# Convolution and 2x2 maximum on one core: head rows through casting loads, joint row sums, and another program order

## The chip, the core and the metric

One of the eight cores of a Trainium2 chip runs the kernel. Its engines work side by side, each through its own queue in order: PE (TensorE, products into PSUM; PEld is its weight load), DVE (VectorE), ACT (ScalarE), POOL (GpSimd) and SP (SyncE, which here only starts transfers). A wait at the head of a queue holds up all that stands behind it on that engine. The metric is the device time of one execution in microseconds (us), the median of several runs.

## What is computed

A 3x3 convolution with padding 1 over 16 images of 64 channels and 64x64 points, to 128 channels, in float32, and then the maximum over 2x2 blocks:

```python
batch, c_in, h, w, c_out, k = 16, 64, 64, 64, 128, 3
conv[b, co] += weight[co, ci, kh, kw] * x_pad[b, ci, kh:kh+h, kw:kw+w]      # for all ci, kh, kw
output[b, c, i, j] = np.max(conv[b, c, 2*i:2*i+2, 2*j:2*j+2])
```

## The kernel before

**Tiling.** Two images lie one above the other in the 128 partitions (2 x 64 channels), so there are 8 image pairs p. A pair's 64 rows are cut into 4 quarters q of 16 rows. A step s is one (p, q): 32 steps, in the sequence of the string `PLACES` (L38). A step gives, for each of its two images (half h = 0 or 1), 8 rows of the output; all its even convolution rows together fill one PSUM bank of 128 x 512 float32 (8 rows of 64), its odd ones another. The input lies in SBUF as bfloat16, in one tile `xb` per pair with a zero row above and below (L81).

**Arithmetic.** For the pair of output rows that a pooling block needs, the three kernel rows g0, g1, g2 are combined beforehand into seven blocks of weights (`BLOCKS`, L104: D2 = g2-g1, G0, D0 = g0-g1, G2, GM = (g0+g2-g1)/2, G1, GP = (g0+g2+g1)/2), each with three taps along the row. The blocks are made on DVE, ACT and POOL (steps D2, D0, g0, g1, g2, GS, GM, GP, and `u..`, which repeats a slot), turned by PE (`T..`, 3 or 4 transposes each) and copied out of PSUM (`V..`). A step of type K (4 of 32) uses 5 blocks on input rows (PA1, PA2, PB1, PB2) and on a row sum S (PR). A step of type W uses 4 (P2 on a row difference E, P0 and P3 on differences D two rows apart, P1 on the row sum S). Each product is three matmuls, one per tap, per half; the halves use different 64 rows of PE and are issued tap by tap in turn (`product`, L220 on). In all 834 matmuls, of which the first K step and the first W step issue their products in two parts of half width (F and G).

**The life of a step.** Bank a takes P2 or PA1; ACT copies it to bank b (SE, W only), and both receive further products; ACT copies bank a into SBUF (EV, negated for W); DVE takes the maximum of bank b and that copy, in place (MX); PE adds the product on the row sum, common to both rows (PR or P1); ACT copies the odd columns to SBUF (OD); DVE takes the maximum of the even columns and these (CM) into the tile `o`, and when both halves are there SP stores it, 256 KB. Eight banks serve all steps, dealt out by the string `BANKS`.

**Who does the row work.** S always on DVE (31 of them L274, the first W step's by a reduce, L265). E (128x512) on POOL for the steps in `E_ON_GPSIMD` (20), else on DVE (L284). D (128x1024) on DVE for those in `D_ON_VECTOR` (16), else on POOL (L294). The first W step has Ea, Eb on DVE (L305) and Da, Db on POOL (L319).

**What sets the order.** The schedule is manual: the string `ORDER` lists every step of every kind once, and each engine's queue is that list with the other engines' entries left out. `product` holds a half until its partner comes. `on_gpsimd` (L73) makes a POOL tensor operation wait for the last DVE operation marked `on_vector` that stands before it in `ORDER`; these are the ones between SBUF tiles, not MX and CM, which work on PSUM. Nothing makes DVE wait for POOL in this way.

**Loads.** SP starts the weights (288 KB) and then, as float32, rows 0 to 16 of pair 0 (`kfirst`, two parts), rows 0 to 16 of pair 1 (`wfirst`, two parts) and rows 17 to 32 of pair 0 (`ksecond`), L86 to L95. DVE casts `kfirst` to `xb` (XOa, XOb, XEa, XEb, L380), ACT `ksecond` (X1, X2, L385); the first W step reads `wfirst` as float32. All later rows come through POOL's queue by DMAs that cast to bfloat16 on the way (`load`, L328: `L.p.lo.hi` is rows lo to hi of pair p). The profile gives the size that these write; they read twice as much. POOL also makes the identity for the transposes (L97), at the very start. The pools have 10 buffers for d, ev and od and 8 for e, s and o.

Of the kernel before, what the change touches and what calls it, by code (L numbers as in the profile page):

```python
# [11 lines left out]
def kernel(  # L12
# [24 lines left out]
    TYPES = "KWKWKWWKWWWWWWWWWWWWWWWWWWWWWWWW"  # L37
    PLACES = "0415267389abcdefghijklmnopqrstuv"  # L38
    E_ON_GPSIMD = (5, 6, 9, 11, 13, 14, 15, 16, 18, 19, 20, 21, 23, 25, 26, 27, 28, 29, 30, 31,)
    D_ON_VECTOR = (3, 5, 9, 10, 11, 13, 15, 16, 18, 19, 20, 21, 23, 26, 27, 29,)  # L40
# [6 lines left out]
    d_pool = ctx.enter_context(tc.tile_pool(name="d_pool", bufs=10))  # L47
    e_pool = ctx.enter_context(tc.tile_pool(name="e_pool", bufs=8))
    s_pool = ctx.enter_context(tc.tile_pool(name="s_pool", bufs=8))
    ev_pool = ctx.enter_context(tc.tile_pool(name="ev_pool", bufs=10))  # L50
    od_pool = ctx.enter_context(tc.tile_pool(name="od_pool", bufs=10))
    o_pool = ctx.enter_context(tc.tile_pool(name="o_pool", bufs=8))
# [4 lines left out]
    acc = [psum.tile([128, R, W], FP32, name=f"acc_{i}") for i in range(8)]  # L57
# [5 lines left out]
    first_cast = []  # L63
# [18 lines left out]
    FAR = 2 * R + 1  # L82
    MID = R + 1
# [3 lines left out]
    assert place[FIRST_K] == (0, 0) and place[FIRST_W] == (1, 0)  # L87
    kfirst = const.tile([128, FAR, W], FP32)
    nc.sync.dma_start(out=kfirst[:, 0:MID, :], in_=rows_of(0, 0, MID))
    nc.sync.dma_start(out=kfirst[:, MID:FAR, :], in_=rows_of(0, MID, FAR))  # L90
    wfirst = const.tile([128, FAR + 1, W], FP32)
    nc.sync.dma_start(out=wfirst[:, 1 : MID + 1, :], in_=rows_of(1, 0, MID))
    nc.sync.dma_start(out=wfirst[:, MID + 1 : FAR + 1, :], in_=rows_of(1, MID, FAR))
    ksecond = const.tile([128, 2 * R, W], FP32)
    nc.sync.dma_start(out=ksecond, in_=rows_of(0, FAR, FAR + 2 * R))  # L95
    ident = const.tile([128, 128], BF16)
    make_identity(nc, ident)  # L97
    nc.vector.memset(wfirst[:, 0, :], 0.0)
# [11 lines left out]
    for s in range(0, GM, 4):  # L110
        nc.gpsimd.memset(wq[:, s, :], 0.0)
# [13 lines left out]
    def ring(m):  # L125
        s = BLOCKS[m]
        nc.gpsimd.tensor_copy(out=wq[:, s + 3, :], in_=wq[:, s, :])

    def turned_cols(m):
        lo = BLOCKS[m] - (m not in RING)  # L130
        hi = BLOCKS[m] + 3
        tp = acc[turned[(m,)]].rearrange("p a b -> p (a b)").bitcast(BF16)
        return lo, hi, tp[:, 0 : (hi - lo) * CO]
# [11 lines left out]
    def turn_out(m):  # L145
        lo, hi, src = turned_cols(m)
        dst = wt[:, lo:hi, :].rearrange("p a b -> p (a b)")
        if m == "GM":
            nc.scalar.mul(dst, src, 0.5)
        elif m == "GP":  # L150
            nc.vector.tensor_scalar_mul(out=dst, in0=src, scalar1=0.5)
        elif m in ("G0", "G2"):
            nc.scalar.copy(out=dst, in_=src)
        else:
            nc.vector.tensor_copy(out=dst, in_=src)

# [5 lines left out]
    def taps(t, h, m0, rows, start=False, skip=None, span=(0, R)):  # L162
# [7 lines left out]
        def one(kw):  # L170
            o0, o1, c0, c1 = (0, W, 0, W) if kw == 1 else (1, W, 0, W - 1) if kw == 0 else (0, W - 1, 1, W)
            if start and kw == 1:
                unset.discard(t)
            nc.tensor.matmul(  # L174
                acc[t][:, i0:i1, o0:o1],
# [85 lines left out]
    def row_sum(s):  # L261
        row["s", s] = s_pool.tile([128, R, W], BF16, name="s")
        if s == FIRST_W:
            with nc.allow_low_precision("bf16 operand of TensorE, as the other row sums"):
                nc.vector.tensor_reduce(  # L265
                    out=row["s", s],
                    in_=wfirst[:, 1 : 1 + 2 * R, :].rearrange("p (r two) w -> p r w two", two=2),
                    axis=mybir.AxisListType.X,
                    op=ADD,
                )  # L270
            return
        t, f = rows_at(s)
        on_vector(
            nc.vector.tensor_tensor(  # L274
                out=row["s", s], in0=t[:, f : f + 2 * R : 2, :], in1=t[:, f + 1 : f + 2 * R : 2, :], op=ADD
            )
        )

    def row_e(s):
        row["e", s] = e_pool.tile([128, R, W], BF16, name="e")  # L280
        t, f = rows_at(s)
        engine, note = (nc.gpsimd, on_gpsimd) if s in E_ON_GPSIMD else (nc.vector, on_vector)
        note(
            engine.tensor_tensor(  # L284
                out=row["e", s], in0=t[:, f : f + 2 * R : 2, :], in1=t[:, f + 1 : f + 2 * R : 2, :], op=SUB
            )
        )

    def row_d(s):
        row["d", s] = d_pool.tile([128, 2 * R, W], BF16, name="d")  # L290
        t, f = rows_at(s)
        engine, note = (nc.vector, on_vector) if s in D_ON_VECTOR else (nc.gpsimd, on_gpsimd)
        note(
            engine.tensor_tensor(  # L294
                out=row["d", s], in0=t[:, f + 1 : f + 1 + 2 * R, :], in1=t[:, f - 1 : f - 1 + 2 * R, :], op=SUB
            )
        )

    def e_half(part):
        s = FIRST_W  # L300
        if part == 0:
            row["e", s] = e_pool.tile([128, R, W], BF16, name="e")
        lo, hi = 1 + R * part, 1 + R * (part + 1)
# [3 lines left out]
                in0=wfirst[:, lo:hi:2, :],  # L307
                in1=wfirst[:, lo + 1 : hi : 2, :],
# [4 lines left out]
    def d_half(part):  # L313
        s = FIRST_W
        if part == 0:
            row["d", s] = d_pool.tile([128, 2 * R, W], BF16, name="d")
        lo, hi = 1 + R * part, 1 + R * (part + 1)
        on_gpsimd(
            nc.gpsimd.tensor_tensor(  # L319
                out=row["d", s][:, R * part : R * (part + 1), :],  # L320
                in0=wfirst[:, lo + 1 : hi + 1, :],
                in1=wfirst[:, lo - 1 : hi - 1, :],
# [4 lines left out]
    def load(p, lo, hi):  # L327
        inst = nc.gpsimd.dma_start(out=xb[p][:, lo + 1 : hi + 1, :], in_=rows_of(p, lo, hi))  # L328
        if first_cast:
            behind(inst, first_cast.pop())  # L330
# [3 lines left out]

    def evac(s, h):
        ev[s, h] = ev_pool.tile([128, R, W], FP32, name="ev")
        t = ta.pop((s, h))
        if TYPES[s] == "K":
            nc.scalar.copy(out=ev[s, h], in_=acc[t])  # L339
        else:  # L340
            nc.scalar.mul(ev[s, h], acc[t], -1.0)  # L341

    def seed(s, h):
        t = take(tb, s, h)
        assert t not in unset
        nc.scalar.copy(out=acc[t], in_=acc[ta[s, h]])  # L346

    def seed_half(part, h):
# [4 lines left out]
        nc.scalar.copy(out=acc[tb[s, h]][:, span, :], in_=acc[ta[s, h]][:, span, :])  # L353

    def rowmax(s, h):
        t = acc[tb[s, h]]
        nc.vector.tensor_tensor(out=t, in0=t, in1=ev[s, h], op=MAX)  # L357

    def odd(s, h):
        od[s, h] = od_pool.tile([128, R, WO], FP32, name="od")  # L360
        nc.scalar.copy(out=od[s, h], in_=acc[tb[s, h]][:, :, 1::2])  # L361

    def colmax(s, h):
        if s not in ot:
            ot[s] = o_pool.tile([128, 2, R, WO], FP32, name="o")
        t = tb.pop((s, h))
        nc.vector.tensor_tensor(out=ot[s][:, h], in0=acc[t][:, :, 0::2], in1=od[s, h], op=MAX)  # L367
        made[s] = made.get(s, 0) + 1
        p, q = place[s]
        dst = out[2 * p : 2 * p + 2, :, q * R : (q + 1) * R, :].rearrange("b c h w -> c b (h w)")  # L370
        src = ot[s].rearrange("p b h w -> p b (h w)")
        if s == LAST:
            store = nc.scalar if made[s] == 1 else nc.sync
            store.dma_start(out=dst[:, h : h + 1], in_=src[:, h : h + 1])
        elif made[s] == 2:
# [3 lines left out]
    def cast_first(lo, hi):  # L379
        inst = nc.vector.tensor_copy(out=xb[0][:, lo + 1 : hi + 1 : 2, :], in_=kfirst[:, lo:hi:2, :])  # L380
        on_vector(inst)
        return inst

    def cast_second(first):
        nc.scalar.copy(out=xb[0][:, FAR + 1 + first : FAR + 1 + 2 * R : 2, :], in_=ksecond[:, first::2, :])  # L385

    steps = {
        "g0": lambda: nc.scalar.copy(out=slots(G0), in_=g0),
        "g1": lambda: nc.scalar.copy(out=slots(G1), in_=g1),
        "g2": lambda: nc.scalar.copy(out=slots(G2), in_=g2),  # L390
        "D2": lambda: on_vector(nc.vector.tensor_sub(out=slots(D2), in0=g2, in1=g1)),
        "D0": lambda: on_vector(nc.vector.tensor_sub(out=slots(D0), in0=g0, in1=g1)),  # L392
        "GS": lambda: on_gpsimd(nc.gpsimd.tensor_tensor(out=gsum, in0=g0, in1=g2, op=ADD)),  # L393
        "GM": lambda: on_vector(nc.vector.tensor_sub(out=slots(GM), in0=gsum, in1=g1)),
        "GP": lambda: on_vector(nc.vector.tensor_add(out=slots(GP), in0=gsum, in1=g1)),
        "XOa": lambda: first_cast.append(cast_first(1, MID)),
        "XOb": lambda: cast_first(MID, FAR),
        "XEa": lambda: cast_first(0, MID),
        "XEb": lambda: cast_first(MID + 1, FAR),
        "X1": lambda: cast_second(0),  # L400
        "X2": lambda: cast_second(1),
# [4 lines left out]
        "Da": lambda: d_half(0),  # L406
        "Db": lambda: d_half(1),
        "SEa": lambda h: seed_half(0, h),
        "SEb": lambda h: seed_half(1, h),
        "S": row_sum, "E": row_e, "D": row_d, "L": load,  # L410
        "SE": seed, "EV": evac, "MX": rowmax, "OD": odd, "CM": colmax,
    }
    for m in BLOCKS:
        steps["u" + m] = lambda m=m: ring(m)
        steps["T" + m] = lambda m=m: turn(m)
        steps["V" + m] = lambda m=m: turn_out(m)
    for m in PRODUCTS:
        steps[m] = lambda s, h, m=m: product(m, s, h)

    ORDER = """  # L420
        D2 TD2 g0 D0 g1 GS TG0 VD2 XOa g2 GM TD0 GP uG1 L.1.15.33 VG0 XOb TG2 VD0 XEa F.0.0 uGM F.1.0 uGP
        L.1.33.64 F.1.1 TGM XEb VG2 F.2.0 F.0.1 F.3.1 S.0 TG1 VGM Ea G.0.0 Eb EV.0.0 L.0.33.64 TGP L.2.0.33
# [102 lines left out]
```

## Time and profile before

| | us |
|---|---|
| median of 3 runs (106.31 to 107.02) | 106.39 |
| the profiled execution, time | 107.13 |
| its span, first to last instruction | 105.2 |
| first product (L174) in the span | 5.54 |
| wraw landed, first weight operation | 3.52 |
| last products end | 100.5 |

The page's first part gives the busy time of each engine, its share of the span and its instructions. A row of the timeline reads: start, duration, engine, line, operation, tiles out<-in, shape, count, and in brackets the idle time ahead of it and what ended that. Durations of neighbouring rows overlap a little, so the pitch, start to start, is what a queue pays. The row of a tile (`s<-xb`) gives minimum, median and maximum in ns. In the chain of work that ended last a row is start, duration, engine and line. "DMA ... us" is from issue to landing.

### The profile page before, as it was taken

To read this page: it belongs to the slowest core of one execution; us is meant where nothing else is said; L and a number is where in the kernel's file an instruction comes from. 1 tells how busy PE (TensorE), PEld (TensorE's weight loads), DVE (VectorE), ACT (ScalarE), POOL (GpSimd) and SP (SyncE) were. 2 spreads that over 40 slices of the span, in tenths; PEclk is the share of its full clock that TensorE was granted. 3 is DMA by queue.
4 is the path that set the end of the run, shared out by engine and by line. 5 is a ranking of instruction groups with operands and counts; after the bars stand their busy time and mean duration, and the time that the engine had idled before them with its cause. 6 is when DMAs were issued, how large, how long until landed. Compare 5 with 4: busy or idle time off the path is not lost.

```text
span 105.2 us, 2469 instructions
## 1 busy us (share of the span) xinstructions
PE 95.9 (91%) x867; PEld 55.1 (52%) x867; DVE 95.4 (91%) x214; ACT 87.0 (83%) x195; POOL 56.8 (54%) x58
## 2 busy tenths in 40 slices
PE   7989999999994999969999999999999999999910
PEld 2457764754562564525545785765554565555400
DVE  2699989999999999999999999989999999869950
ACT  4648677688786599949999999999999999999830
POOL 4298661924857345937157754479484483843000
PEclk9999999999999999999999999999999999999995
DMA  2999999999999994289898994032340514222061
GB/s 77 285 364 161 205 209 212 230 224 220 224 223 221 253 374 162 80 120 190 173 360 127 206 295 156 0 109 100 138 159 20 184 43 162 100 100 100 6 241 61
DMA packets 11037, 18.09 MB, mean 172 GB/s; under 512 B 784, under 2 KB 8976, under 8 KB 10384
## 3 DMA queue, kind: packets, MB, share of 16 engines
q0 software_dynamic: 1440, 7.60, 38.9%
q1 hardware_dynamic: 9440, 10.19, 28.2%
q8 instruction: 7, 0.11, 0.4%
q10 hardware_dynamic: 144, 0.13, 0.4%
q14 instruction: 6, 0.05, 0.2%
HBM read 17.14 MB, written 8.39 MB: 243 GB/s over the span
## 4 chain that ended last, share of the span: by engine, by line
PE 49%; ACT 8%; DVE 4%; issue 3%; DVEq 0%; ACTq 0%
PE acc L174 49%; ACT acc L346 5%; ACT ev L341 3%; DVE acc L357 2%; DVE o L367 1%; ACT od L361 1%; DVE s L274 1%; DVEq L520 0%; ACTq L346 0%; DVEq L367 0%
## 5 line engine op out<-in xcount | busy, mean ns | idle before, releaser
L174 PEld LDWEIGHTS <-wt 64*128 64x128 bf16 x834 | 52.7, 94 | 40.9 <-issue 12.4
L174 PE MATMUL acc<-d,wt 64*128 64x512 bf16 (+2 forms) x348 | 68.4, 369 | 1.2 <-ACT acc L346 1.0
L174 PE MATMUL acc<-s,wt 64*128 64x504 bf16 (+1 forms) x192 | 45.9, 376 | 0.2 <-DVE acc L357 0.2
L357 DVE TENSOR_TENSOR acc<-acc,ev 128x512 f32<-128x512 f32 x64 | 42.5, 691 | 1.7 <-ACT ev L341 0.7
L174 PE MATMUL acc<-e,wt 64*128 64x512 bf16 (+3 forms) x174 | 41.5, 369 | 1.9 <-DVE o L367 1.9
L346 ACT COPY acc<-acc 128x512 f32<-128x512 f32 x54 | 31.8, 597 | 4.8 <-PE acc L174 2.5
L284 POOL TENSOR_TENSOR e<-xb 128x512 bf16<-128x512 bf16 x20 | 23.0, 1155 | 22.9 <-PE acc L174 9.0
L341 ACT ACTIVATE ev<-acc 128x512 f32<-128x512 f32 x56 | 33.5, 614 | 1.9 <-PE acc L174 1.2
L294 POOL TENSOR_TENSOR d<-xb 128x1024 bf16<-128x1024 bf16 x11 | 23.5, 2136 | 12.2 <-DVE e L284 2.9
L367 DVE TENSOR_TENSOR o<-acc,od 128x256 f32<-128x256 f32 x64 | 25.3, 416 | 1.6 <-ACT od L361 1.1
L361 ACT COPY od<-acc 128x256 f32<-128x256 f32 x64 | 23.4, 383 | 3.6 <-PE acc L174 3.1
L174 PE MATMUL acc<-xb,wt 64*128 64x504 bf16 (+7 forms) x120 | 16.7, 332 | 0.5 <-DVE xb L380 0.5
L274 DVE TENSOR_TENSOR s<-xb 128x512 bf16<-128x512 bf16 x31 | 16.5, 558 | 0.0
L294 DVE TENSOR_TENSOR d<-xb 128x1024 bf16<-128x1024 bf16 x16 | 10.9, 682 | 0.0
L328 POOL DMA_DIRECT2D xb<-in_x_dram x10 | 5.7, 574 | 0.2 <-issue 0.2
L339 ACT COPY ev<-acc 128x512 f32<-128x512 f32 x8 | 4.8, 612 | 0.3 <-PE acc L174 0.3
L483 PE MATMUL acc<-const-bfloat16-1.0 128*128 128x512 bf16 x8 | 3.4, 600 | 0.8 <-PEq L506 0.8
L284 DVE TENSOR_TENSOR e<-xb 128x512 bf16<-128x512 bf16 x7 | 2.9, 417 | 0.0
L319 POOL TENSOR_TENSOR d<-wfirst 128x512 bf16<-128x512 f32 x2 | 2.5, 1267 | 0.3 <-DVE e L305 0.3
L393 POOL TENSOR_TENSOR gsum<-wraw 128x192 f32<-128x192 f32 x1 | 0.8, 816 | 2.8 <-DVE wq L392 2.8
L483 PEld LDWEIGHTS <-const-bfloat16-1.0 128*128 128x128 bf16 x8 | 1.0, 137 | 2.4 <-issue 2.4
L139 PE MATMUL acc<-ident,wq 128*128 128x128 bf16 x25 | 2.2, 220 | 0.0
(29 smaller groups left out, 18.9 us busy)
## 6 DMA issues: line engine op xcount, KB each, us to landing
out_dram<-o SPq DMA_DIRECT2D x31, 256.0 KB, 3.1
xb<-in_x_dram POOLq DMA_DIRECT2D x5, 1024.0 KB, 15.0
xb<-in_x_dram POOLq DMA_DIRECT2D x3, 496.0 KB, 9.0
xb<-in_x_dram POOLq DMA_DIRECT2D x1, 528.0 KB, 11.0
ksecond<-in_x_dram SPq DMA_DIRECT2D x1, 512.0 KB, 5.8
wraw<-in_weight_dram SPq DMA_DIRECT2D x1, 288.0 KB, 2.7
kfirst<-in_x_dram SPq DMA_DIRECT2D x1, 288.0 KB, 3.6
wfirst<-in_x_dram SPq DMA_DIRECT2D x1, 288.0 KB, 4.8
```

What stands on the lines that cost most here:

```text
L174: nc.tensor.matmul(acc[t][:, i0:i1, o0:o1], wt[lo : lo + CI, tap_of(m0, kw, h), :], rows(lo, i0, i1, c0, c1), start=start and kw == 1, sto ...
L274: nc.vector.tensor_tensor(out=row["s", s], in0=t[:, f : f + 2 * R : 2, :], in1=t[:, f + 1 : f + 2 * R : 2, :], op=ADD)
L284: engine.tensor_tensor(out=row["e", s], in0=t[:, f : f + 2 * R : 2, :], in1=t[:, f + 1 : f + 2 * R : 2, :], op=SUB)
L294: engine.tensor_tensor(out=row["d", s], in0=t[:, f + 1 : f + 1 + 2 * R, :], in1=t[:, f - 1 : f - 1 + 2 * R, :], op=SUB)
L328: inst = nc.gpsimd.dma_start(out=xb[p][:, lo + 1 : hi + 1, :], in_=rows_of(p, lo, hi))
L339: nc.scalar.copy(out=ev[s, h], in_=acc[t])
L341: nc.scalar.mul(ev[s, h], acc[t], -1.0)
L346: nc.scalar.copy(out=acc[t], in_=acc[ta[s, h]])
L357: nc.vector.tensor_tensor(out=t, in0=t, in1=ev[s, h], op=MAX)
L361: nc.scalar.copy(out=od[s, h], in_=acc[tb[s, h]][:, :, 1::2])
L367: nc.vector.tensor_tensor(out=ot[s][:, h], in0=acc[t][:, :, 0::2], in1=od[s, h], op=MAX)
L483: nc.tensor.matmul(acc[n].rearrange("p a b -> p (a b)"), ones[:, 0:128], ones, start=True, stop=True, skip_group_check=True)
```

## The change

1. `kfirst`, `wfirst`, `ksecond`, their loads and the casts are gone. Five casting loads L.0.0.9, L.0.9.17, L.1.0.17, L.0.17.33, L.1.17.33 stand first in `ORDER`; the identity (`ID`) comes behind them on POOL. Ea, Eb, Da, Db read `xb`. The zero slots of `wq` are set by DVE.
2. Steps of `ORDER` can carry two marks. `+` picks the other engine: for D, Da, Db, the raw blocks g0..g2 and GS it means DVE, for E it means POOL, for `u` it means ACT, and for `V` it swaps ACT and DVE. It takes the place of `E_ON_GPSIMD` and `D_ON_VECTOR`. `&` makes one operation of two: S& and E& work on a step and its neighbour quarter (q and q^1 of the same pair; 1024 elements a partition), MX& and CM& on both halves of a step.
3. Row sums and differences live in tiles for two quarters, `ev` and `od` in tiles for both halves, all banks in one PSUM tile `acc`. `SWAPPED` says for which steps the halves lie in changed places; these are stored in two DMAs.
4. `load` and `ring` on POOL now go through `on_gpsimd` too: every POOL load waits for the DVE operation between SBUF tiles that stands before it.
5. Other pool sizes: d 8, e 6, s 6 (now two quarters each), ev 7, od 7 (now both halves each), o 6.
6. A new `ORDER`, `BANKS` and, with steps 6 and 7 exchanged in places, `PLACES` and `TYPES` (the K steps are now 0, 2, 6, 14).

In the new order: S 6 single and 13 joint; E on DVE 3 single and 4 joint, on POOL 4 single and 6 joint; D 12 on DVE and 15 on POOL; CM joint for two steps, MX never.

```diff
-    TYPES = "KWKWKWWKWWWWWWWWWWWWWWWWWWWWWWWW"
-    PLACES = "0415267389abcdefghijklmnopqrstuv"
...
+    TYPES = "KWKWWWKWWWWWWWKWWWWWWWWWWWWWWWWW"
+    PLACES = "0415263789abcdefghijklmnopqrstuv"
...
-    def ring(m):
+    def ring(m, alt):
         s = BLOCKS[m]
-        nc.gpsimd.tensor_copy(out=wq[:, s + 3, :], in_=wq[:, s, :])
+        dst, src = wq[:, s + 3, :], wq[:, s, :]
+        if alt:
+            nc.scalar.copy(out=dst, in_=src)
+        else:
+            on_gpsimd(nc.gpsimd.tensor_copy(out=dst, in_=src))
...
+    def half_pair(of, pool, s):
+        p, q = place[s]
+        key = of, p, q // 2
+        if key not in pair_tiles:
+            pair_tiles[key] = pool.tile([128, 2 * R, W], BF16, name=of)
+        t = pair_tiles[key]
+        lo = R * (q % 2)
+        row[of, s] = t[:, lo : lo + R, :]
+        return t, lo
...
+    def row_pairs(s, joint):
         t, f = rows_at(s)
...
+        n = 2 * R
+        if joint:
+            f, n = min(f, rows_at(neighbour(s))[1]), 4 * R
+        return t[:, f : f + n : 2, :], t[:, f + 1 : f + n : 2, :]
+
+    def combine(of, pool, op, s, joint, on_pool):
+        t, lo = half_pair(of, pool, s)
+        dst = t[:, lo : lo + R, :]
+        if joint:
+            half_pair(of, pool, neighbour(s))
+            dst = t
+        in0, in1 = row_pairs(s, joint)
+        engine, note = (nc.gpsimd, on_gpsimd) if on_pool else (nc.vector, on_vector)
+        note(engine.tensor_tensor(out=dst, in0=in0, in1=in1, op=op))
...
     def load(p, lo, hi):
-        inst = nc.gpsimd.dma_start(out=xb[p][:, lo + 1 : hi + 1, :], in_=rows_of(p, lo, hi))
-        if first_cast:
-            behind(inst, first_cast.pop())
+        on_gpsimd(nc.gpsimd.dma_start(out=xb[p][:, lo + 1 : hi + 1, :], in_=rows_of(p, lo, hi)))
...
     ORDER = """
-        D2 TD2 g0 D0 g1 GS TG0 VD2 XOa g2 GM TD0 GP uG1 L.1.15.33 VG0 XOb TG2 VD0 XEa F.0.0 uGM F.1.0 uGP
-        L.1.33.64 F.1.1 TGM XEb VG2 F.2.0 F.0.1 F.3.1 S.0 TG1 VGM Ea G.0.0 Eb EV.0.0 L.0.33.64 TGP L.2.0.33
-        S.1 EV.0.1 F.3.0 F.2.1 SEa.1 SEa.0 VG1 Da VGP MX.0.1 MX.0.0 Db X1 L.2.33.64 G.0.1 L.3.0.64 X2 PA1.2.1
-        D.3 G.1.0 PA2.2.1 SEb.0 SEb.1 PA1.2.0 G.2.0 G.1.1 PR.0.0 S.3 EV.1.0 E.5 G.2.1 EV.1.1 PB1.2.1 OD.0.0
-        E.3 EV.2.1 PA2.2.0 MX.1.0 PR.0.1 S.2 PB2.2.1 P2.3.0 P2.3.1 OD.0.1 PB1.2.0 EV.2.0 CM.0.0 P1.1.0 MX.1.1
...
+        L.0.0.9 L.0.9.17 L.1.0.17 g2 L.0.17.33 L.1.17.33 g1 D2 D0 ID GS+ uG1+ TD2 TG2 g0+ VD2+ GM TD0 GP TG1
+        TG0 F.0.0 VD0+ L.0.33.64 uGM+ F.2.0 uGP+ VG2 VG1 TGM PA1.2.1 TGP F.0.1 L.1.33.64 VGP+ VG0+ S.0 Eb Ea
+        F.1.1 PA2.2.1 F.1.0 Db+ Da+ F.3.0 F.3.1 VGM EV.0.0 S.1 G.0.0 S.2 EV.0.1 F.2.1 SEa.1 SEa.0 G.0.1 SEb.0
+        L.2.0.33 MX.0.1 MX.0.0 L.3.0.64 PA1.2.0 G.1.0 SEb.1 G.1.1 EV.1.1 G.2.1 E.3 PR.0.1 G.2.0 PR.0.0 EV.1.0
+        D+.3 S.3 OD.0.0 MX.1.1 CM.0.0 EV.2.1 L.2.33.64 P2.3.0 PA2.2.0 D+.4 OD.0.1 PA1.6.0 CM.0.1 P1.1.1 SE.3.0
+        P0.3.0 PB1.2.1 E+.4 OD.1.1 PA2.6.0 P3.3.0 MX.1.0 CM.1.1 PB1.6.0 EV.2.0 P2.3.1 S&.6 EV.3.0 PB2.2.1
+        PB2.6.0 D+.5 SE.3.1 P2.4.1 EV.6.0 P0.3.1 D+.7 P3.3.1 MX.2.1 SE.4.1 E+.7 P1.1.0 MX.3.0 EV.3.1 P0.4.1
+        P3.4.1 P2.4.0 MX.6.0 OD.1.0 PR.6.0 PR.2.1 MX.3.1 EV.4.1 SE.4.0 CM.1.0 L.4.0.64 P1.3.0 E&+.9 OD.2.1
+        P1.3.1 MX.4.1 OD.6.0 CM.2.1 OD.3.0 OD.3.1 P0.4.0 PA1.6.1 CM.6.0 PB1.2.0 P1.4.1 P2.7.1 EV.4.0 OD.4.1
+        P3.4.0 SE.7.1 PA2.6.1 E.5 CM.3.1 CM.3.0 P2.5.1 PB2.2.0 CM.4.1 D.9 P2.5.0 EV.6.1 P2.8.0 MX.4.0 P0.7.1
+        P1.4.0 MX.2.0 D+.8 SE.5.1 P3.7.1 EV.7.1 E&.13 S&.7 MX.7.1 L.5.0.64 PR.2.0 SE.5.0 P0.5.1 OD.4.0 P3.5.1
+        P1.7.1 CM.4.0 OD.2.0 P0.5.0 P3.5.0 P2.7.0 EV.5.1 CM.2.0 EV.5.0 P2.9.1 SE.8.0 OD.7.1 MX.5.1 P0.8.0
+        MX.5.0 P3.8.0 CM.7.1 D.11 SE.9.1 SE.7.0 P1.5.1 E&.10 EV.8.0 D+.10 S&.9 P0.9.1 EV.9.1 OD.5.1 P1.5.0
...
```

## The prediction, made before the result

> **What bounds the kernel now.** I read the busy times first, then the chain of work that ended last, then the timeline around its gaps, then the landings of the loads.
>
> ```profile
> PE 95.9 (91%) x867; PEld 55.1 (52%) x867; DVE 95.4 (91%) x214; ACT 87.0 (83%) x195; POOL 56.8 (54%) x58
> ```
>
> PE and DVE both look full, so an average cannot say which binds. PE runs 834 products; 84 are half wide, which leaves 792 full ones. In the ten-microsecond windows of the weight-load row 90 to 92 of them pass in the good stretches, but 74 in 30:40 and 78 in 40:50. At 92 per 10 us, 792 cost 86 us; the 25 transposes are worth about 1.5; PE's products lie between 5.54 and 100.5, 95 us. So some 7.5 us of PE's stretch is idle. The chain names one place, the timeline two more:
>
> ```profile
> 43.42 0.70 DVE acc L357
> 44.12 0.59 DVE s L274
> 44.71 0.33 issue
> 45.04 0.02 DVEq L367
> 45.06 0.80 issue
> 45.86 0.42 DVE o L367
> ...
> 46.98 4.48 PE acc L174 x36
> ```
>
> ```profile
> 30.91 2.68 DVE L274 TENSOR_TENSOR s<-xb 128x512 bf16<-128x512 bf16 x2
> 31.08 2.24 POOL L294 TENSOR_TENSOR d<-xb 128x1024 bf16<-128x1024 bf16 x1 [1.07 <-DVE d L294]
> ...
> 33.85 0.74 DVE L367 TENSOR_TENSOR o<-acc,od 128x256 f32<-128x256 f32 x2
> ...
> 34.32 1.17 PEld L174 LDWEIGHTS <-wt 64*128 64x128 bf16 x12 [1.97 <-issue]
> ```
>
> ```profile
> L274 DVE TENSOR_TENSOR s<-xb x31: 409/418/2346, 7.5 to 97.4; 128x512 bf16<-128x512 bf16 x31
> ```
>
> The third fence, minimum, median and maximum in ns, says that a row sum S costs 418 ns but once 2346. In the second fence S meets a D on POOL (started 31.08): the two S take 2.68 instead of 0.75, the colmax behind them is late, and PE stands still for 1.97 until the bank is free. In the first, an S at 44.03 runs 1.91 beside a POOL E at 44.48, and PE idles 1.34 before 46.98. A third S, at 14.12, takes 1.39 beside a POOL E that began 14.08. The three overruns (1.93, 1.49, 0.97) sum to 4.4 us, all of the excess of S's mean of 558 ns. Two-input SBUF work of DVE and POOL thus excludes each other here, and who comes second waits.
>
> **The change, part by part.**
>
> Prices below: pitches of back-to-back rows. MX 0.60 (four in 2.48), CM 0.335 (three in 1.07), S or E 0.335 (four in 1.42), D on DVE 0.60, POOL E 1.155 and D 2.13, POOL DMA issue 0.57.
>
> *Joint sums.* 32 S become 6 single and 13 joint. A joint S writes 1024 elements a partition, like a D: 0.60 against 2 x 0.335. S costs 6 x 0.335 + 13 x 0.60 = 9.8 against 31 x 0.335 + 1.23 (the reduce on wfirst) = 11.6. DVE's E: 3 single, 4 joint = 3.4 against 2.3. DVE's D: 12 x 0.60 = 7.2 against 9.6, and Da, Db come to DVE, 2 x 0.335 = 0.7. Together 21.1 against 23.5, -2.4 us of DVE. Only two CM are joint, -0.1. No joint form is in the trace: D bounds it above, two singles would cost 0.67. POOL: 4 x 1.155 + 21 x 2.13 + 14 x 0.57 = 57.3 beside the 52.2 of the same three rows before. On the path: DVE is later than PE only in places, so 0 to -2.4; I take -0.3.
>
> *The order and the rule.* Both kernels hold a POOL tensor operation behind the DVE SBUF operation before it in the order; nothing holds DVE back, so what counts is how much PSUM-side DVE work (MX, CM) the order puts between. Counting MX and CM at their pitches: before, POOL's D.14 has 0.0 us between D.10 and S.11 (the stall at 30.91), E.20 has 0.0 between S.14 and S.13 (44.03), E.5 0.0 before E.3. After: E+.4 (1.15) gets 1.27; E+.7 + L.4 + E&+.9 (3.85) get 4.01; D.9 (2.13) 2.21; L.5 + D.11 (2.70) 2.81; L.6 + E+.15 + D.17 (3.85) 4.01; D.12 + L.7 + D.19 (4.83) 5.28; D.18 2.21; D.22 2.47. Four are too small on paper: D.16 + E&+.19 (4.26 against 3.74), D.21 + E+.23 (3.28, 3.14), E&+.27 + D.27 (4.26, 3.74), D.28 (2.13, 1.87), 1.4 us of overlap if DVE never idles. So PE's 1.97 and 1.34 go; for the overrun at 14.12 PE idled 0.75 at 15.9, of which I count 0.5: -3.8. Ends: 0 if POOL slips out of its windows, -3.8 plus the remaining 3.7 of PE's idle time at best. Behind the stall comes ACT: the chain from 51.47 to 55.59 is ACT, and DVE's leftover overlap comes back, so I give back 0.7: -3.1. Loads now also wait behind DVE work: L.0.33.64 and L.1.33.64 behind GP (near 6 us), L.2.0.33 and L.3 behind S.2, L.4 behind D+.7 in DVE and E+.7 in POOL's queue. At each the queue still holds a load's worth of bytes, so 0.
>
> *Head.* SP issues only wraw; five casting loads go first on POOL, 5 x 0.57 to 0.70 from 0.74, so the identity ends near 4.1 (before 1.3). TD2 waits for it and for D2 (4.02 before): cover just enough, 0. The four XO/XE casts (1.4 us of DVE pitch) and X1, X2 on ACT (1.1) go. F.0.0 needed the first cast (idle 0.16); now it needs VD2 on ACT, behind g2, g1 and uG1: 3.52 + 0.43 + 0.44 + 0.3 + 0.58 = 5.3, and TG0, which waits for g0 on DVE behind D2, D0 and GS: 5.2, plus four transposes to 5.5. So near 5.6 against 5.54. wraw no longer has the transfer engines to itself:
>
> ```profile
> 3.52 0.50 DVE L391 TENSOR_TENSOR wq<-wraw 128x192 bf16<-128x192 f32 x1 [1.93 <-DMA wraw<-in_weight_dram]
> ...
> 5.80 0.70 POOL L328 DMA_DIRECT2D xb<-in_x_dram  x1 [0.22 <-issue]
> ```
>
> The second line is the first POOL load of all: 0.70, near the usual 0.57, so a cold one costs 0.13 more. For wraw the bounds are 0 (its 288 KB still first) and +1.0 (another 288 KB beside it at the 292 GB/s of that microsecond); I take +0.4, as the POOL load's issue ends some 0.2 after SP's. Then PE gets F and G through with Da, Db on DVE (0.7) instead of POOL (2.5): about -0.4. Head in sum 0, from -0.7 to +1.0. The Trainium skill, DMA: Bandwidth & Descriptors, section "Issuing engines are not separate DMA queues", says that DMAs of all issuing engines interleave on the same 16 engines; by it wraw is late by about the full 1.0 and the sum 0.6 higher; no run shown yet has two queues at the start.
>
> *Early loads.* Rows in source bytes: 1888 KB were down at 8.9 (ksecond, 3.08 + 5.8), 3456 at 14.0 (L.1.33.64, 6.84 + 7.1), 8544 at 26.7 (L.3). On that curve the new order gets L.1.0.17 at 7.6, L.1.17.33 near 10.8, L.0.33.64 near 13.6, L.1.33.64 near 16.2, L.3 near 24.1, L.2.33.64 near 26.6. DVE, summed from S.0 at about 7.5, reaches D+.4 near 12.8, D+.5 near 15.3, E&.13 near 24.2, E&.10 near 27.6. D+.4 and D+.5 come up to 0.9 early; behind them on DVE stand MX.1.0 and MX.2.1, for which P1.1 and PR.2 wait. +0.6, from 0 to +2.
>
> *Tail and pools.* The last products, odd, colmax and store are the same in number; the 4.7 us after 100.5 stay. Fewer o and d buffers (6, 8): six steps of 2.7 us cover the 16.7 us that stores took in 10:20 barely; 0, up to +0.5. Thirteen steps with swapped halves issue two stores instead of one; SP is idle, 0. Ring copies and three turn-outs go to ACT, g0 and VG0 to DVE: ACT +0.6 against 83% busy, 0.
>
> **Sum** in the profiled execution: -0.3 - 3.1 + 0 + 0.6 = -2.8; of the smaller idle times (16 to 18, 51 to 56, 96 to 100, some 3 us) I take another -0.6, because DVE has 2.4 us less to do: -3.4. The span of 105.2 becomes 101.8; with the 1.93 around it (107.13 - 105.2) 103.7. That execution stood 0.74 over the median 106.39, so 103.0.
>
> **Rivals.**
> A. The collisions only move: POOL reaches its windows late (it waits for a buffer or a load) and meets joint S and E, whose wait is as long and blocks two steps. For it: POOL's D rise from 11 to 15, and four windows are too small. Against it: the loads' issue time is reserved in the windows. Two collisions with PE idle of 1.97 each give back 3.9: 106.4 + 0.5 = 106.9, within 1%.
> B, the other side. The casting loads carry the head too slowly. Between 8.9 and 11.4, with the casting queue taking over, 576 KB took 2.5 us, 230 KB/us. If everything from 1.9 us ran so, the 4384 KB up to L.1.33.64 would be down at 21.9 instead of 16.2; D+.5 stands in DVE's queue from 15.3, and MX, CM behind it free the eight banks, so PE stops for 5.7 less about 1 of work in hand: +4.7, and the gain of 3.4 is 1.3 lost: 107.7. It decides once L.1.33.64 lands later than 16.2 + 1 + 3.4 = 20.6. For it: 1 us windows of 134 to 182 GB/s (written) at 9 to 11. Against it: from 14.0 on 383 KB/us. The Trainium skill, SBUF — State Buffer, in the box on the "DVE blocks DMA" trap of the section "SBUF: two separate sides", has POOL's descriptor writing starved while DVE runs two-port operations, which would do the same; the trace's ten POOL issues lie between 0.53 and 0.70, so it does not show it.
> C. The order is worse in itself: PE waits for banks all along, at 88 instead of 92 products per 10 us over 80 us: +3.6, less 3.1: 106.9; at 86, +5.6 less 3.1: 108.9. For it: before's tail and 50:60 (87) show such waits without a collision. Against it: 60:90 runs at 90 to 92.
> D. All idle time but 1.5 us goes: PE ends near 94.5, 99.2 + 1.9 - 0.7 = 100.4.
>
> **How the numbers follow.** Forecast 0.50 (101.2 to 105.2), D 0.09, A 0.15, B 0.11, C 0.15. A measurement of this kernel tells about 1% from no change. Faster: forecast, D and a little of C, 0.60; same: A and some of C, 0.16; slower: B and the rest, 0.24. The range reaches from D's 100.2 to 107.9, past B's price; the likeliest one's own is 101.2 to 105.2.
>
> **What would show it.** S, joint or not, with a maximum below 0.9 us; no weight-load gap over 1 us between 28 and 50; windows of 30:40 and 40:50 with 88 or more; first product at 5.5 to 6.1; wraw's wait ending by 4.0; D+.5 waiting for a load less than 1 us. Wrong: POOL operations under way when a joint S or E starts and DVE rows over 1.5 us; DVE waiting for xb loads after 15 us for more than 2 us; a first product after 6.5.

## The result, and the profile after

| | before | after |
|---|---|---|
| median, us | 106.35 (4 runs, 106.25 to 107.02) | 114.53 (4 runs, 113.31 to 116.28) |
| profiled execution, time / span, us | 107.13 / 105.2 | 114.51 / 112.7 |

The ratio is 1.072, 95% interval 1.062 to 1.082: slower, where 103.0 was forecast, and outside the range. A median here and below is over all executions, a ratio and its interval leave out those more than 1.5% above the fastest of their kernel. First the page of the changed kernel: busy times, then busy tenths in 40 slices of 2.8 us, with the granted clock of PE and the share of the DMA engines.

```profile
PE 97.6 (87%) x867; PEld 57.7 (51%) x867; DVE 88.9 (79%) x197; ACT 87.7 (78%) x197; POOL 57.8 (51%) x45
...
PE   7796899999993086999999999997999999999920
...
DVE  3756899999991042969999899996998897879950
...
PEclk9999999999999855589999999999999999999995
DMA  3999999999999995507989140122522223232052
```

DVE has shed 6.5 us (95.4 to 88.9), close to the sum of the 2.4 and of the 4.4 of overruns that the prediction names, and yet the end is later. The loss stands in one place: from 34 to 40 us PE and DVE are nearly empty, DVE stays thin for two slices more, and PE's clock falls. The chain of work that ended last goes through that place (start, duration, engine and line):

```profile
23.39 0.68 DVE o L398 x2
24.09 0.33 SPq L408
24.42 0.04 issue
24.46 19.67 DMA out_dram<-o
44.13 0.03 issue
44.16 0.05 DVEq L398
44.21 0.04 issue
44.25 0.77 DVE o L398 x2
45.02 0.04 issue
45.06 31.42 PE acc L178 x269
```

A store of 128 KB, issued at 24.46, is on its way for 19.67 us, and a column maximum (CM, L398) cannot write before it has landed: the tile `o` that CM wants is still being read. The timeline of DVE shows two such waits, in brackets; that of the weight loads what PE made of them:

```profile
32.31 1.88 DVE L385 TENSOR_TENSOR acc<-acc,ev 128x512 f32<-128x512 f32 x3
39.20 0.69 DVE L394 TENSOR_TENSOR o<-acc,od 128x512 f32<-128x512 f32 x1 [5.02 <-DMA out_dram<-o]
39.93 0.70 DVE L385 TENSOR_TENSOR acc<-acc,ev 128x512 f32<-128x512 f32 x1
44.25 1.08 DVE L398 TENSOR_TENSOR o<-acc,od 128x256 f32<-128x256 f32 x3 [3.62 <-DMA out_dram<-o]
```

```profile
39.95 0.13 PEld L178 LDWEIGHTS <-wt 64*128 64x128 bf16 x3 [5.62 <-issue]
40.33 0.17 PEld L178 LDWEIGHTS <-wt 64*128 64x128 bf16 x2 [0.25 <-issue]
...
45.06 0.13 PEld L178 LDWEIGHTS <-wt 64*128 64x128 bf16 x3 [1.60 <-issue]
...
48.43 3.65 PEld L178 LDWEIGHTS <-wt 64*128 64x128 bf16 x33 [0.25 <-issue]
```

PE stands still for 5.62 and 1.60 us, and between 39.95 and 48.43 it takes two matmuls per 0.43 us where it takes four otherwise (33 in 3.65). The place where before had its collisions is clean: no row sum is long any more.

```profile
L296 DVE TENSOR_TENSOR s<-xb x19: 415/680/783, 6.7 to 103.1; 128x1024 bf16<-128x1024 bf16 x13, 128x512 bf16<-128x512 bf16 x6
```

It is useful to cut an execution in three: the head, up to the first product on a row sum; the body, to the end of the last product; the tail. PE's timeline gives the first mark; the second is the start of the last copy OD in the chain, right behind the last products. Each row is one execution, the profiled one.

| kernel | head ends | products end | body | span |
|---|---|---|---|---|
| before | 12.27 | 100.5 | 88.2 | 105.2 |
| after | 13.74 | 107.5 | 93.8 | 112.7 |
| e1_o8 | 14.47 | 99.9 | 85.4 | 105.0 |
| e2_o12 | 14.24 | 98.6 | 84.4 | 104.5 |
| e3_l6_late | 16.12 | 104.5 | 88.4 | 110.5 |
| e11_fewloads | 14.03 | 98.6 | 84.6 | 104.0 |
| e5_split | 14.85 | 97.5 | 82.6 | 102.6 |
| e7_plainhead | 12.88 | 95.5 | 82.6 | 100.4 |

### The profile page after: what moved, and what is told of

The parts are those of the page before. It is cut to its first block, busy times and chain, and to the rows that moved or that the text cites. A ratio compares the mean times of both kernels' runs of the same rounds, so it can differ in the third digit from the quotient of the medians.

```text
span 112.7 us, 2454 instructions
## 1 busy us (share of the span) xinstructions
PE 97.6 (87%) x867; PEld 57.7 (51%) x867; DVE 88.9 (79%) x197; ACT 87.7 (78%) x197; POOL 57.8 (51%) x45
## 4 chain that ended last, share of the span: by engine, by line
PE 61%; DMA 23%; DVE 6%; ACT 3%; issue 1%; POOL 1%; DVEq 0%; SPq 0%; ACTq 0%; POOLq 0%
PE acc L178 61%; DMA out_dram<-o 17%; DMA xb<-in_x_dram 6%; DVE o L398 3%; DVE acc L385 2%; POOL xb L345 1%; ACT acc L374 1%; ACT acc L381 1%; ACT od L389 1%; DVE o L394 1%; ACT ev L369 0%; DVE e L320 0%; SPq L408 0%; DVE e L296 0%; DVEq L556 0%
## 5 line engine op out<-in xcount | busy, mean ns | idle before, releaser
L178 PEld LDWEIGHTS <-wt 64*128 64x128 bf16 x834 | 55.2, 96 | 45.2 <-issue 18.4
L178 PE MATMUL acc<-d,wt 64*128 64x512 bf16 (+2 forms) x348 | 70.8, 376 | 0.4 <-ACT acc L381 0.4
L309 POOL TENSOR_TENSOR d<-xb 128x1024 bf16<-128x1024 bf16 x15 | 31.9, 2130 | 21.0 <-DVE s L296 14.6
L398 DVE TENSOR_TENSOR o<-acc,od 128x256 f32<-128x256 f32 x60 | 23.7, 416 | 5.7 <-DMA out_dram<-o 3.6
L296 POOL TENSOR_TENSOR e<-xb 128x1024 bf16<-128x1024 bf16 (+1 forms) x10 | 17.4, 1741 | 9.0 <-DVE d L309 5.3
L178 PE MATMUL acc<-xb,wt 64*128 64x504 bf16 (+6 forms) x120 | 20.6, 350 | 0.0
L345 POOL DMA_DIRECT2D xb<-in_x_dram x14 | 7.8, 562 | 12.0 <-DVE s L296 9.8
L296 DVE TENSOR_TENSOR s<-xb 128x1024 bf16<-128x1024 bf16 (+1 forms) x19 | 11.2, 603 | 0.2 <-DMA xb<-in_x_dram 0.2
L309 DVE TENSOR_TENSOR d<-xb 128x1024 bf16<-128x1024 bf16 x12 | 8.1, 680 | 0.0
L394 DVE TENSOR_TENSOR o<-acc,od 128x512 f32<-128x512 f32 x2 | 1.4, 692 | 6.0 <-DMA out_dram<-o 5.0
L296 DVE TENSOR_TENSOR e<-xb 128x1024 bf16<-128x1024 bf16 (+1 forms) x7 | 4.2, 597 | 0.0
```

The lines of the kernel that those rows point to most:

```text
L178: nc.tensor.matmul(acc[:, t, i0:i1, o0:o1], wt[lo : lo + CI, tap_of(m0, kw, h), :], rows(lo, i0, i1, c0, c1), start=start and kw == 1, sto ...
L296: note(engine.tensor_tensor(out=dst, in0=in0, in1=in1, op=op))
L309: engine.tensor_tensor(out=row["d", s], in0=t[:, f + 1 : f + 1 + 2 * R, :], in1=t[:, f - 1 : f - 1 + 2 * R, :], op=SUB)
L345: on_gpsimd(nc.gpsimd.dma_start(out=xb[p][:, lo + 1 : hi + 1, :], in_=rows_of(p, lo, hi)))
L398: nc.vector.tensor_tensor(out=o[:, k], in0=acc[:, tb[s, h], :, 0::2], in1=od[s][:, k], op=MAX)
```

## The experiments

The theory after the result (T): the casting loads keep the transfer engines full up to 44 us, so stores land late; six `o` tiles are then too few, and DVE, in order, holds everything up behind a CM. Rivals: the order itself is bad (R1); the order merely holds the tiles too long, whatever the stores do (R2); the head is the loss (R3).

### e1_o8 and e2_o12: more o tiles

```diff
-    o_pool = ctx.enter_context(tc.tile_pool(name="o_pool", bufs=6))
+    o_pool = ctx.enter_context(tc.tile_pool(name="o_pool", bufs=8))    # e1; 12 in e2
```

> The changed kernel with 8 buffers for o, as before had, instead of 6. Store theory (two colmax wait 5.0 and 3.6 us for o buffers whose stores took 16.9 and 19.7 us to land; PE idles 5.6 and 1.6 us behind them and then runs at half clock): the ninth tile takes the first store's buffer, landed by 28, the tenth that of a store landed by 39; the first wait goes, at most 1 to 2 us of a second stays: 103.5 to 106. Order theory (the order itself starves PE, the store wait only shows it): another wait takes its place, 110 or more.

> The changed kernel with 12 buffers for o. Store theory: no colmax waits for a store, no idle time of PE over 2 us, granted clock 0.98 or more, and the gain of the forecast comes out: 102 to 104.5. Order theory: 107 or more with PE waiting for banks. Collision part of the forecast: S and E on DVE have maxima below 0.9 us as in the changed kernel.

Measured: 107.65 (ratio to before 1.003, 0.995 to 1.011) with 8, 105.86 (0.995, 0.990 to 1.000) with 12. The one number 6 thus costs 6.9 us against the 8 that before had, and 8.7 against 12; by the bodies it is 8.4 and 9.4. R1 and R3 fall as causes of the loss. With 8, in ten executions between 105.80 and 109.09, the profiled one (106.74) has one wait left, in DVE's timeline:

```profile
38.68 0.42 DVE L398 TENSOR_TENSOR o<-acc,od 128x256 f32<-128x256 f32 x1 [1.04 <-DMA out_dram<-o]
```

With 12 there is none. But 105.86 is still 2.9 above the forecast and above the 104.5 that the expectation allowed. In e2's timeline of the weight loads two gaps stand out:

```profile
35.81 3.76 PEld L178 LDWEIGHTS <-wt 64*128 64x128 bf16 x36 [0.98 <-issue]
...
69.03 2.50 PEld L178 LDWEIGHTS <-wt 64*128 64x128 bf16 x25 [1.12 <-issue]
```

Both end with one of the two joint CM (L394, at 35.06 and 68.28 us).

### e3_l6_late and e11_fewloads: loads later, and loads left out

e3 moves L.6.0.64 to the place of L.7.0.64 (behind D.12) and that one behind D.16. e11 leaves the loads of pairs 5 and 6 out; their steps read the rows of pairs 0 and 1, so their part of the output is not the convolution. Both have 6 `o` tiles.

```diff
-... MX.7.1 L.5.0.64 PR.2.0 ...          # e11
+... MX.7.1 PR.2.0 ...
-        L.6.0.64 P3.9.1 P0.7.0 ...
+        P3.9.1 P0.7.0 ...
-        return xb[p], 2 * R * q + 1
+        return xb[{5: 0, 6: 1}.get(p, p)], 2 * R * q + 1
```

> The changed kernel, 6 buffers for o, with the load of pair 6 issued where that of pair 7 stood, and pair 7's behind D.16: the loads then pause after pair 5's landing (38.5 in the changed kernel) instead of running to 43.8. Store theory with starvation by loads: the stores issued at 24 land near 38.5 to 39.5 instead of 44.1; the second wait (3.6 us) goes, the first (to 39.2) stays about as it is: 108 to 111. If stores are slow whatever the loads do: 113 to 115.

> The changed kernel as it is, with 6 o buffers, but the loads L.5.0.64 and L.6.0.64 are left out, and the steps of pairs 5 and 6 read the rows of pairs 0 and 1 in their place (that part of the output is left out by this). All else is in the same order. If the waits for o buffers at 34 and 41 us come from stores that share the transfer engines with the casting loads, the stores issued from 22 us on land when L.4 is done at 33 or soon after, at most 12 us after issue, the two store waits shrink from 5.0 and 3.6 to under 1 together, and the time is 105.5 to 108. Rival: the new order holds six o tiles so long that even quick stores do not free one in time; then the waits stay and the time is 112 to 115.

Measured: e3 112.34 (ratio 1.054, 1.047 to 1.061), above the 108 to 111 that T expected; e11 105.95 (0.997, 0.992 to 1.002), as good as twelve tiles, with a single wait for a store, of 0.45 at 53.22. The landing times of the stores issued between 20 and 26 us (in the answers on tile `o` for that window), in the order before, changed kernel, e3, e11:

```profile
DMA to landing us min/median/max: 14.9/16.3/17.7
```

```profile
DMA to landing us min/median/max: 12.0/18.3/19.8
```

```profile
DMA to landing us min/median/max: 9.3/9.3/9.3
```

```profile
DMA to landing us min/median/max: 9.4/10.2/11.1
```

With L.6 late the stores land in half the time and the first wait, 5.02, is gone; L.5, still there, lands at 41.33, and one wait is left:

```profile
41.84 0.42 DVE L398 TENSOR_TENSOR o<-acc,od 128x256 f32<-128x256 f32 x1 [2.54 <-DMA out_dram<-o]
```

That e3 is slow all the same lies in good part ahead of the body, which is 5.4 shorter than after's: in the profiled execution the head ends at 16.12, 2.4 later than after's. PE stood there for 1.97 and 0.65 us, and its clock was 0.50 from 12 to 15 us, as the page's row shows (slices of 2.8 us; the second dip follows the wait at 41.84):

```profile
PEclk9999679999999996799999999999999999999995
```

Six tiles in the same order are enough once the stores land in 10 us instead of 18. R2 falls: the hold times alone do no harm. But they count: in e11 the second half of step 6 gets its CM at 38.03, 15 us after the first, and so one of the six tiles is away for that time before its store is even issued.

### e4_before_o6: six o tiles in the kernel before

```diff
-    o_pool = ctx.enter_context(tc.tile_pool(name="o_pool", bufs=8))
+    o_pool = ctx.enter_context(tc.tile_pool(name="o_pool", bufs=6))
```

> The kernel before with 6 buffers for o instead of 8, nothing else. Store theory: its stores took 15.1 to 18.3 us when issued between 16.8 and 21, so the seventh tile, wanted near 25, waits for a store issued at 16.8 that lands at 31.9: PE idles some 5 us and the clock falls: 111 to 116. Order theory: buffers do not matter, 106 to 107.

Measured: 108.81 (1.019, 1.012 to 1.026), less than expected. The old order loses 2.3 us by six tiles (before is 106.47 beside it), the new one 8.7. One wait is there, 1.84 at 30.31, and PE stands 1.71. Its stores issued between 16 and 24 us took 14.2 to 19.6, about as long as after's, so slow stores alone do not cost 8.7 either: that takes slow stores together with the new order. What differs behind them: before, L.5 landed at 37.3 and L.6 was issued only at 43.88, and the stores behind it landed from 37.6 on; after, L.6 is issued at 32.7 and lands at 43.8, and most stores behind it land at 43.9 and later.

### e5_split: the two joint CM taken apart

```diff
-... EV.14.1 CM&.5.0 P1.9.1 ...      ... P3.20.1 CM&.19.0
+... EV.14.1 CM.5.0 CM.5.1 P1.9.1 ...      ... P3.20.1 CM.19.0 CM.19.1
```

(on top of e2_o12)

> The changed kernel with 12 buffers for o and both joint colmax (CM&.5, CM&.19) taken apart into two single ones in the same place. Theory (the joint colmax holds two banks until both halves are ready: PE idles 0.98 us before 35.8 and 1.12 us before 69.0): both go, 103.5 to 104.8. Rival (PE would wait there anyway, for ACT): no change from e2_o12, 105.5 to 106.3.

Measured: 104.54 (0.982, 0.978 to 0.987), 1.3 less than e2. The chain of e5 has one piece of PE from 13.96 to 92.29:

```profile
13.96 78.33 PE acc L178 x718
```

Both gaps of e2 are gone; that the joint CM made them is shown. How it did so is my reading: it waits for the later of its two halves, and takes 0.69 where the first of two single ones is done in 0.42, so that the bank of the earlier half comes free late. It had been costed at -0.1.

### e6_before_nocoll: the old kernel without its collisions

Five steps of the old order are moved, nothing else:

```diff
-... P1.6.1 D.14 S.11 OD.6.1 PB2.7.0 S.9 E.10
+... P1.6.1 S.11 OD.6.1 PB2.7.0 S.9 E.10 D.14
-        E.20 SE.13.0 P1.11.1 P3.12.0 S.13 EV.12.0
+        SE.13.0 P1.11.1 P3.12.0 S.13 E.20 EV.12.0
-... EV.1.0 E.5 G.2.1 ...      ... S.2 PB2.2.1
+... EV.1.0 G.2.1 ...          ... S.2 E.5 PB2.2.1
```

> The kernel before with nothing changed but the places of five steps in its order, so that the three collisions of DVE and POOL are gone: S.11, S.9, E.10 ahead of D.14; S.13 ahead of E.20; E.5 behind S.2. The forecast's main term by itself: -2 to -3.8 us, 102.7 to 104.5, S with a maximum below 0.9 us, no weight-load gap over 1 us between 28 and 50. Rival (PE's idle time comes back as waits for ACT or banks): 105.5 to 106.7.

Measured: 104.97 (0.986, 0.982 to 0.990), -1.43, between what theory and rival expected; the body falls from 88.2 to 85.7. No row sum is above 428 ns (2346 before):

```profile
L274 DVE TENSOR_TENSOR s<-xb x31: 411/418/428, 7.8 to 95.1; 128x512 bf16<-128x512 bf16 x31
```

Part comes back: a gap of 1.41 at 38.65, where PE waits for a CM, is new.

### e7_plainhead, e8_id_early, e9_best: the head

e7 (on top of e5) brings rows 0 to 16 of pair 1 as float32 through SP again, for Ea, Eb, Da, Db and S.1:

```diff
+    wfirst = const.tile([128, 2 * R + 2, W], FP32)
+    nc.sync.dma_start(out=wfirst[:, 1 : R + 2, :], in_=rows_of(1, 0, R + 1))
+    nc.sync.dma_start(out=wfirst[:, R + 2 : 2 * R + 2, :], in_=rows_of(1, R + 1, 2 * R + 1))
...
-        L.0.0.9 L.0.9.17 L.1.0.17 g2 L.0.17.33 L.1.17.33 g1 ...
+        L.0.0.9 L.0.9.17 g2 L.0.17.33 L.1.15.33 g1 ...
```

e8 (on top of e5) puts ID ahead of L.1.0.17; e9 (on top of e7) puts ID ahead of L.0.17.33 and lets ACT store the first half of the last step.

> e5_split with the head rows of pair 1 loaded as before: as float32 by SP in two parts, read as float32 by Ea, Eb, Da, Db and S.1; POOL's first loads are L.0.0.9, L.0.9.17, L.0.17.33, L.1.15.33. Theory (the casting loads bring L.1.0.17 down only at 9.1 to 9.6 and hold the first E and what follows by some 1 us): Ea starts near 7.6 to 8.0, 0.5 to 1.2 us faster than e5_split. Rival (the same 16 engines carry the same bytes, nothing gained, and float32 sources cost DVE some 1 us more): 0 to +1.

> e5_split with the identity made on POOL ahead of the third load instead of behind the fifth. Theory (PE's first transpose waited 0.4 to 0.7 us for it): the first product comes 0.3 to 0.7 earlier, but the first E still waits for L.1.0.17, issued 0.7 later: 0 to +0.5 in all. If the transposes set the head: -0.5.

> The kernel of e7_plainhead (12 o buffers, both joint CM taken apart, head rows of pair 1 as float32 by SP: 103.09) with two more edits: the identity is made ahead of the third transfer, and the last step's first half is stored by ACT and not by SP. If the theory holds that the head is bound by the landings of rows and that the tail after the last product (some 5 us) holds one transfer issue too many on SP, the first edit gives 0 to -0.3 and the second 0 to -0.5: 102.3 to 103.1. Rival: both places are hidden behind the landing of the last store, 103.1 to 103.5.

Measured: e7 103.09 (0.970, 0.964 to 0.975), the fastest; e8 104.21 (0.978, 0.972 to 0.983) against e5's 104.54, within the intervals; e9 103.33 (0.971, 0.963 to 0.978), no difference to e7. So the identity and the last store make no measurable difference, and the way in which pair 1's first rows come does: 1.45 us. In DVE's timeline Ea and Eb start at 10.20 in e5, behind a wait for the load, and at 7.62 in e7 with none:

```profile
10.20 0.49 DVE L320 TENSOR_TENSOR e<-xb 128x256 bf16<-128x256 bf16 x2 [2.78 <-DMA xb<-in_x_dram]
```

```profile
7.62 0.75 DVE L326 TENSOR_TENSOR e<-wfirst 128x256 bf16<-128x256 f32 x2
```

### e10_single and e12_collide: joint sums and one collision, priced

e10 (on top of e7) takes every S& and E& of DVE apart; e12 (on top of e7, with 8 `s` buffers) moves one S& beside a D on POOL:

```diff
-... P2.3.1 S&.6 EV.3.0 ...            # e10, 17 places
+... P2.3.1 S.6 S.4 EV.3.0 ...
-... MX.9.0 D.12 L.7.0.64 P0.11.0 ...      ... S&.18 S&.12 ...            # e12
+... MX.9.0 D.12 S&.18 L.7.0.64 P0.11.0 ...      ... S&.12 ...
```

> The kernel of e7_plainhead with all 17 joint operations of DVE (13 S, 4 E) taken apart, each into two single ones in the same place. Prices the joint sums. A joint one costs 0.68 to 0.69 in its row, two single ones 2 x 0.42, some 0.07 more in pitch each, so DVE does 1.2 us more. If PE binds from 12 to 90 us, as the unbroken chain of e7_plainhead says, 103.1 to 103.6 against 103.09. Rival: DVE is close behind PE everywhere, and the 1.2 us come out in full: 104.2 to 104.5.

> The kernel of e7_plainhead with one joint row sum moved: S&.18 stands right behind D.12, which is on GpSimd, in place of behind D.19 (and 8 s buffers, so that no buffer is waited for). Nothing else changes. If two-input SBUF work of VectorE and GpSimd excludes each other, S&.18 waits for D.12: its row goes from 0.69 to 2.0 to 2.8 us, the MX behind it are late, and PE stands still for 0.5 to 2 once: 103.6 to 105.1. The old kernel lost 1.97 and 1.34 of PE's time at such places. Rival: PE has work in the banks to cover a single stall of 2 us here, 103.0 to 103.4.

Measured: e10 103.94 (0.978, 0.973 to 0.984), 0.85 above e7 and between the two expectations, while the intervals of e7 and e10 still overlap; the body grows from 82.6 to 83.3. e12 104.68 (0.989, 0.984 to 0.993), 1.6 above e7; the body grows by 1.6, to 84.2. DVE and POOL at that place of e12, then its weight loads:

```profile
39.67 2.12 POOL L315 TENSOR_TENSOR d<-xb 128x1024 bf16<-128x1024 bf16 x1 [2.84 <-DVE s L302]
...
40.65 1.70 DVE L302 TENSOR_TENSOR s<-xb 128x1024 bf16<-128x1024 bf16 x1
42.27 1.88 DVE L391 TENSOR_TENSOR acc<-acc,ev 128x512 f32<-128x512 f32 x3
```

```profile
43.01 0.09 PEld L182 LDWEIGHTS <-wt 64*128 64x128 bf16 x1 [0.70 <-issue]
43.60 0.33 PEld L182 LDWEIGHTS <-wt 64*128 64x128 bf16 x5 [0.51 <-issue]
```

The S ends 0.56 after the D (42.35 and 41.79): its work is done behind D, 1.0 us later than without it (1.70 against 0.69), and PE loses it in gaps of 0.70, 0.51 and 0.46, the last at 45.18. That a collision costs more than its own wait, 1.6 against 1.0, was seen in this one case.

## Why the prediction was wrong, step by step

- **Tail and pools** is the step that failed: "six steps of 2.7 us cover the 16.7 us that stores took in 10:20 barely; 0, up to +0.5". Six times 2.7 is 16.2, so by its own numbers they did not cover it. It cost 6.9 against the 8 tiles of before and 8.7 against twelve (after against e1 and e2). Three things were missing. The landing time was taken from before, but the same change pulls L.6 forward by 11 us, and with it stores issued at 24 us take 19.8, not 14.9; with L.6 late (e3) the stores of that window take 9.3. A tile is away not from its store on but from the first CM of its step: 19.8 and some 4 us from the first CM to the store (0.5 to 6 in steps 0 to 4), over 2.7 us per step, asks for 8.8 tiles, as an estimate; 8 left one wait, 12 none. And the price of running out is not the shortfall: the CM at the head of DVE's queue holds up every S, E, D and MX behind it, so PE stood for 7.2 us and ran at half clock for 7.0 more. "Barely" should have been a rival with a price, not a term of 0.
- **Early loads**, "+0.6": the loads were weighed for landing late, never for what they do to the stores. No D on DVE waited for rows, so the +0.6 did not come. But L.6 early is part of the loss: with it late the body falls from 93.8 to 88.4 (e3), with L.5 and L.6 left out to 84.6 (e11).
- **The order and the rule**, "-3.1": right in kind, its size not shown. S has a maximum of 783 ns after; removing the collisions in the old kernel alone gives -1.43 (body -2.5); putting one back costs 1.6. One row does not fit "who comes second waits": the S at 44.03 starts 0.45 ahead of the E at 44.48. What all four collisions share is the end: the S ends 0.27 to 0.56 after the POOL operation. In e5 and e7, the chain is one piece of PE from the head to 90 us, and the body is 5.6 shorter than before's. That is one execution each: before's profiled one is 0.8 over its median and e7's 0.9 under, and by the medians e7 gains 3.3 in all. Together with the other terms of the body (-0.3, +0.6, -0.6) I had -3.4; e2, with the joint CM still in, has -3.8.
- **Joint sums**, "-0.3": +0.85 when taken apart (e10), body +0.7; the sign is right, and the size is low by half or more if the difference is real. Joint CM, in "-0.1", cost 1.3 (e2 against e5).
- **Head**, "0, from -0.7 to +1.0": its end moves from 12.27 to 13.74 after, 14.24 in e2, 14.85 in e5, so +1.5 to +2.6. wraw, for which I had taken +0.4, ended its wait at 3.52 in both. The Trainium skill, DMA: Bandwidth & Descriptors, section "Issuing engines are not separate DMA queues", says that transfers of all issuing engines interleave on the same 16 engines; the +1.0 for wraw that I had drawn from it is not borne out by that row. The rows of pair 1 were the late ones: forecast 7.6, landed at 9.07 in the chain of after. This is rival B at small size; e7 gained 1.45 by the medians, but its head end, 12.88, is the earliest of those listed at the end.
- **Rivals.** C, "PE waits for banks all along", does not hold: 90 to 95 matmuls per 10 us in e7's windows from 20 to 90. A, "the collisions only move", does not either, by the row of S. None of the four had a tile that waits for a store. B's price was too high by a slip: 4384 KB at 230 KB/us from 1.9 are down at 21.0, not 21.9, which makes it 106.8. The value 103.0 itself is reached by e7, 103.09, after three edits; of that agreement the head's +0.6 and the body's -5.6, against 0 and -3.4, are both misses, so it is in part luck.
- **What would show it**: the maximum of S below 0.9 came true, wraw by 4.0 too; no gap over 1 us between 28 and 50 did not (5.62 and 1.60), nor did 88 in the windows from 30 to 50 (41 and 49), nor the first product by 6.1 (6.22). Of the signs of being wrong none came: no S or E of DVE over 1.5 us, no wait of DVE for rows after 15 us, no first product after 6.5. They watched the collisions and the loads, not the stores.

What stays open: how the gain of the body in e5 and e7 beyond e6's 2.5 and e10's 0.7, some 2.4 us, is split between the rule, the rest of the order and the spread between executions; no run here takes the rule alone.

## What to carry to other kernels

A pool that is made smaller is costed by the longest time that one of its tiles is away, from its first writer to the landing of its store, and with the landing times that the changed kernel will have, not those of the old. If a change moves loads forward, ask which stores wait beside them and who wants their tiles; a wait of an in-order engine for such a tile stops everything behind it. Two operations merged into one wait for the later of their inputs. Here the merge cost on CM, the last operation before a bank comes free (1.3 us for two), and by e10 it paid on row sums, which are early (0.85 for 17, intervals overlapping).

## What the runs showed of the hardware

**Stores starve beside casting loads.** After 60 us a store of the changed kernel lands in 2.1 us (median); between 20 and 26 us, with casting loads queued, in 18.3. The answer on DMA for 34 to 44 us of after, when both kinds were waiting, gives packets, MB and share of the 16 engines' time:

```profile
q0 software_dynamic: 228, 1.61, 76.7%
q1 hardware_dynamic: 731, 0.70, 21.6%
```

A packet of the casting queue (q0) moves 7.1 KB and takes 0.54 us of an engine (76.7% x 16 x 10 / 228), one of the stores (q1) 0.96 KB and 0.047 us. So the stores got 30% of the bytes. The Trainium skill, DMA: Bandwidth & Descriptors, section "Queues, rings and completion order", says that an engine takes turns between queue rows packet by packet. By these packet sizes, as an estimate, turns of one packet each would give stores 0.96 of each 8.1 KB, 12%; the trace has 3.2 store packets to each casting one, so turns of one packet, as the profile counts them, are not what it shows.

Single landings show the waiting better than the shares. In after, stores issued at 21.83, 22.20 and 24.09 land at 33.87, 39.08 and 43.93, each within 0.7 us behind a load (L.4 at 33.18, L.5 at 38.46, L.6 at 43.75). In e3 four stores land from 33.50 to 34.45, behind L.4 at 33.33; in e11 four from 33.20 to 34.11, behind L.4 at 33.02. Why the second and third store of after also wait for loads that were issued behind them is not shown.

**The clock after a stall.** PE's one-microsecond windows in the changed kernel (us, busy, granted clock, DMA share, GB/s):

```profile
38.00:39.00 1.00, 0.00 (x0) 0.69 1.10 238
39.00:40.00 1.00, 0.05 (x2) 0.50 0.99 213
...
47.00:48.00 1.00, 1.00 (x6) 0.50 0.81 262
48.00:49.00 1.00, 1.00 (x10) 0.69 0.00 0
49.00:50.00 1.00, 1.00 (x12) 1.00 0.07 15
```

PE had stopped at 34.3. The clock halves some 4 us into the stall (0.69 in 38:39) and comes back at about 48.6, 3.6 us after PE's second start at 45.06; the 3.5 us of work between the two stalls had not sufficed. At half clock PE did some 7.0 us of work, of which 3.5 is loss: the stalls of 7.2 cost 10.7. The body is 9.4 longer than in e2, which has a gap of 0.98 of its own in that place. The Trainium skill, TensorE: Matmul & The Clock Gate, section "What's actually happening", gives at least one idle and one busy window of about 3.4 us for the two changes; this stall agrees. The head of e3 shows that shorter stalls can do it too: PE had stood for 1.97 and 0.65 us there, with some matmuls between, when the clock fell in the window 11:12 (0.85, then 0.50).

**The head varies.** S.0 in kernels with the same first loads, e7, e12 and e10, starts at 7.28, 8.44 and 8.91 us, each time behind the landing of a casting load, so one execution of each differs by 1.6 us before the body begins. The ends of the head say the same: 12.27, 12.44 and 12.51 with before's loads (before, e4, e6); 12.88, 13.24, 14.05 and 14.97 with e7's (e7, e9, e12, e10); 13.74 to 14.85 with the five casting loads, and 16.12 in e3. This is why the body was compared above.
